# Attention by pairs of heads: logits of two heads in turn, probabilities divided by their sums before they are transposed

## The chip, the core and the metric

One core of a Trainium2 chip runs the whole program in one launch. The metric is the device time of that launch in microseconds, of which lower is better. Three runs of the kernel before took 1363.26, 1365.01 and 1368.75 us, median 1365.01.

## The reference, cut to what matters

Two transformer blocks of two layers each, over 256 tokens of width 1024, in float32. Three of the four mixers are attention with 16 heads of 64 channels:

```python
# causal attention of layer 0 ("moba"; with one block of 256 keys it is plain causal attention)
l = einsum('hqd,hkd->hqk', q, k) * scale
l = where(d >= 0, l + bias_table[bucket(d)], NEG)
o = einsum('hqk,hkd->hqd', softmax(l), v)
# layer 1 ("dsa"): the same, and each query keeps the 64 keys of the highest index score
logits = where(valid, logits + bias, NEG);  p = softmax(logits)
# layer 3, dilated: three branches (window, dilation) = (128,1), (512,4), (2048,16);
# their outputs are joined by their log-sum-exp, so that one softmax over all three holds
```

The rest is matrix products: gated or squared-relu MLPs, a short convolution, projections.

## The kernel before

All weights, 424 chunks of 512 KB, stream from memory in the order of their use (`Stream`, lines 96 to 134). Each chunk holds eight 128x128 tiles. ScalarE (ACT) rounds it to float32r (`wH`, line 121), VectorE (DVE) subtracts to get the rest (`wL`, line 122), in quarters of 128x256. Each product of a tile is then three matmuls (`mm3` and `mm3t`, lines 202 to 214: high by high, high by low, low by high). Matmuls of attention itself are plain float32 (`mm`, line 216), which the trace shows as two records each.

`Kernel.attend` (lines 505 to 530) issues attention as a pipeline over units. A unit is one head in the two causal layers (16 units, class `Causal`) and one head and one half of the queries in the dilated layer (32 units, class `Dilated`). In turn i it issues, in this order: `qk` of unit i (logits, into one PSUM bank of the pool `psB`, which has four), `soft` of unit i, some pieces of background work, `tr` of unit i - lag (three 128x128 transposes on TensorE (PE), and a copy by DVE from PSUM to the tile `ptS`), further pieces, `pv` of unit i - lag - 1 and `fin` of unit i - lag - 2. The background `bg` is the generator of the projections that feed attention and of the output projection that follows it; a table of numbers gives the pieces per turn. One piece is 12 matmuls of a projection, with the weights that they need. A scheduler then fixes each engine's order; instructions of an engine run in that order.

`soft_part` (line 1087) is one DVE instruction that adds the bias, negates, and keeps the row's least value (line 1093), and one `Exp` on ACT that also sums the row (line 1094). The division by that sum comes at the end, for two heads together, since a pair of heads fills the 128 rows of one output tile: `inverses` (line 1106) takes the reciprocals on DVE and spreads them over 64 columns on ACT (line 1112); `pv` (line 1114) transposes them on PE (line 1123), copies them out of PSUM on ACT (line 1125), does the products with the values, multiplies by them on DVE (line 1128, tile `ao`), and splits the result into high and low parts (`split_into`, lines 223 and 224).

The two heads of a pair, e = 0 and 1, have their queries and keys in rows 0 to 63 and 64 to 127 of one tile, so a logits matmul uses 64 rows of the array. `select_keys` (line 783) in layer 1 has such matmuls too: for the second half of the queries two per bank, in the order bank 0 and bank 1 of e = 0, bank 0 and bank 1 of e = 1 (lines 789 to 797).

## Time and profile before

| what | value |
|---|---|
| runs, median | 1365.01 us |
| profiled execution: time of the run | 1363.71 us |
| its span, first to last instruction | 1361.9 us |
| mean granted TensorE clock | 0.991 |
| busy: PE / PE weight loads / DVE / ACT / GpSimd (POOL) | 98% / 90% / 69% / 62% / 1% |
| weight and other DMA traffic | 238.73 MB, 175 GB/s mean |

The profiled execution is one run, so sums over it are set against 1363.71 us, of which 1361.9 us is its span. PE records are pipelined: a record's duration covers its way through the array, and records overlap. What a matmul costs a busy PE is the distance from its start to the next one's start. DVE and ACT records overlap by some 0.08 us in the same way.

### The profile page before, as it was taken

How to read it: one execution, taken by the hardware profiler on the slowest of the kernel's cores; microseconds unless marked ns; L12 is line 12 of the kernel's file. 1: busy time of each engine (PE TensorE's matmuls, PEld its weight loads, DVE VectorE, ACT ScalarE, POOL GpSimd, SP SyncE). 2: the span in 40 equal slices, each digit the busy share in tenths (PEclk: the TensorE clock that was granted, in tenths of full speed). 3: DMA queues.
4: the chain of work that ended last, by engine and by line, in shares of the span. 5: the costliest groups of instructions: out<-in, count | busy, mean ns of one | idle time of the engine just before them, and what ended most of it. 6: DMA issues, size and time to landing. Idle time of an engine off the chain costs nothing.

```text
span 1361.9 us, 27454 instructions
## 1 busy us (share of the span) xinstructions
PE 1335.7 (98%) x10238; PEld 1230.3 (90%) x10238; DVE 946.1 (69%) x2529; ACT 841.2 (62%) x2325; POOL 7.4 (1%) x17
## 2 busy tenths in 40 slices
PE   8899999999999999999999999999999999999998
PEld 6788999999779999999989999888998987899997
DVE  6467866568878656689886666775677777766665
ACT  6466856566767656586675555777655555655554
POOL 0000000000000000000000000000000000000000
PEclk9899999999899999999999999999999999999999
DMA  8933565655224665656656666465755553466662
GB/s 238 267 109 110 171 200 173 203 180 176 92 79 140 192 211 186 203 163 216 203 168 202 196 190 194 152 211 186 222 191 162 156 158 109 142 204 194 192 196 77
DMA packets 67137, 238.73 MB, mean 175 GB/s; under 512 B 8139, under 2 KB 8556, under 8 KB 67004
## 3 DMA queue, kind: packets, MB, share of 16 engines
q1 hardware_dynamic: 65324, 231.30, 54.0%
q0 software_dynamic: 1536, 5.64, 1.8%
q8 instruction: 80, 1.31, 0.4%
q14 instruction: 53, 0.43, 0.1%
q10 hardware_dynamic: 144, 0.06, 0.0%
HBM read 228.83 MB, written 1.84 MB: 169 GB/s over the span
## 4 chain that ended last, share of the span: by engine, by line
PE 92%; DVE 3%; DMA 2%; ACT 2%; issue 0%; DVEq 0%; ACTq 0%
PE A L205 18%; PE A L206 17%; PE A L207 17%; PE B L217 7%; PE B L206 4%; PE B L205 4%; PE B L207 4%; PE B L213 3%; PE B L214 3%; PE B L212 3%; PE A L212 2%; PE A L214 2%; PE A L213 2%; DMA wT<-in_w 2%; PE B L1162 1%; PE B L1204 1%
## 5 line engine op out<-in xcount | busy, mean ns | idle before, releaser
L121 ACT ACTIVATE wH<-wT 128x256 fp32r<-128x256 f32 x1696 | 574.8, 406 | 400.5 <-PE A L206 177.4
L122 DVE TENSOR_TENSOR wL<-wT,wH 128x256 fp32r<-128x256 f32 x1696 | 617.4, 419 | 278.7 <-ACT wH L121 277.4
L205 PE MATMUL A<-Xh,wH 128*128 128x256 f32 x1768 | 492.4, 279 | 0.7 <-DVE x L386 0.7
L206 PE MATMUL A<-Xl,wH 128*128 128x256 f32 x1768 | 491.9, 278 | 0.3 <-DVE Xl L227 0.2
L207 PE MATMUL A<-Xh,wL 128*128 128x256 f32 x1768 | 491.5, 278 | 0.0
L205 PEld LDWEIGHTS A<-Xh,wH 128*128 128x128 f32 x1768 | 333.7, 189 | 3.1 <-ACT Xh L226 1.0
L206 PEld LDWEIGHTS A<-Xl,wH 128*128 128x128 f32 x1768 | 333.7, 189 | 2.1 <-DVE Xl L227 1.0
L207 PEld LDWEIGHTS A<-Xh,wL 128*128 128x128 f32 x1768 | 333.6, 189 | 0.0
L206 PE MATMUL B<-Al,wH 128*128 128x256 f32 x512 | 142.3, 278 | 0.0
L205 PE MATMUL B<-Ah,wH 128*128 128x256 f32 x512 | 142.1, 278 | 0.0
L207 PE MATMUL B<-Ah,wL 128*128 128x256 f32 x512 | 142.1, 278 | 0.0
L205 PEld LDWEIGHTS B<-Ah,wH 128*128 128x128 f32 x512 | 96.2, 188 | 0.0
L206 PEld LDWEIGHTS B<-Al,wH 128*128 128x128 f32 x512 | 96.1, 188 | 0.0
L207 PEld LDWEIGHTS B<-Ah,wL 128*128 128x128 f32 x512 | 95.9, 187 | 0.0
L214 PE MATMUL B<-wL,Fh 128*128 128x512 f32 x176 | 69.4, 394 | 0.0
L213 PE MATMUL B<-wH,Fl 128*128 128x512 f32 x176 | 69.0, 392 | 0.0
L212 PE MATMUL B<-wH,Fh 128*128 128x512 f32 x176 | 68.4, 389 | 0.0
L1094 ACT ACTIVATE pr<-pr,sm 128x128 f32<-128x128 f32 (+1 forms) x96 | 48.1, 501 | 25.4 <-DVE sm L1093 24.7
L205 PE MATMUL A<-XQh,wH 128*128 128x256 f32 x192 | 58.0, 302 | 0.0
L212 PE MATMUL A<-wH,Xh 128*128 128x512 f32 x128 | 51.8, 405 | 5.8 <-ACT wH L121 5.4
L206 PE MATMUL A<-XQl,wH 128*128 128x256 f32 x192 | 53.6, 279 | 0.0
L207 PE MATMUL A<-XQh,wL 128*128 128x256 f32 x192 | 53.4, 278 | 0.0
(252 smaller groups left out, 1700.1 us busy)
## 6 DMA issues: line engine op xcount, KB each, us to landing
wT<-in_w SPq DMA_DIRECT2D x422, 512.0 KB, 3.7
sw<-raw SPq DMA_DIRECT2D x48, 128.0 KB, 2.6
bias<-ud POOLq DMA_DIRECT2D x4, 512.0 KB, 13.6
wT<-in_w SPq DMA_DIRECT2D x4, 256.0 KB, 3.9
out_dram<-xt SPq DMA_DIRECT2D x4, 256.0 KB, 2.4
x<-in_x SPq DMA_DIRECT2D x3, 256.0 KB, 5.9
ud<-us POOLq DMA_DIRECT2D x1, 768.0 KB, 10.2
growfinal_norm<-in_gr POOLq DMA_DIRECT2D x1, 512.0 KB, 5.7
```

What stands on the lines that cost most here:

```text
L121: nc.scalar.activation(h[:, at], t[:, at], AF.Copy)
L122: nc.vector.tensor_tensor(out=lo[:, at], in0=t[:, at], in1=h[:, at], op=ALU.subtract)
L205: mm(out, lhsT=wh, rhs=xh, start=start, stop=False, skip_group_check=True)
L206: mm(out, lhsT=wh, rhs=xl, start=False, stop=False, skip_group_check=True)
L207: self.last = mm(out, lhsT=wl, rhs=xh, start=False, stop=stop, skip_group_check=True)
L212: mm(out, lhsT=xh, rhs=wh, start=start, stop=False, skip_group_check=True)
L213: mm(out, lhsT=xl, rhs=wh, start=False, stop=False, skip_group_check=True)
L214: self.last = mm(out, lhsT=xh, rhs=wl, start=False, stop=stop, skip_group_check=True)
L217: self.nc.tensor.matmul(out, lhsT=lhsT, rhs=rhs, start=start, stop=stop, skip_group_check=True)
L1094: nc.scalar.activation(p, p, AF.Exp, scale=-1.0, bias=mx, accum_out=s["l"][:, i, self.e:self.e + 1])
L1162: K.nc.tensor.transpose(pt[:, i * P:(i + 1) * P], self.p[:, i * P:(i + 1) * P], K.ident[:])
L1204: K.nc.tensor.transpose(pt[:, b * P:(b + 1) * P], self.p[:, b * P:(b + 1) * P], K.ident[:])
```

## The change

Attention goes by pairs of heads. A causal unit is now a pair (8 units); a dilated unit is a pair and one half of the queries (16 units). `qk` takes two banks and issues the two heads' matmuls alternately, e = 0 and 1. The probabilities are multiplied by the reciprocal sums before they are transposed: in the causal layers on DVE, issued one turn after the softmax (`norm_late`), in the dilated layer on GpSimd, issued in the turn of the softmax (`norm_early`). The spread, transposed and copied reciprocals of `inverses` and `pv` and the multiplication into `ao` go; the product's bank is split directly. The first matmul of a product now opens its accumulation. The tables of pieces are rewritten for the longer turns, and causal `pr` tiles have 6 buffers for 4.

```diff
@@ attend
             at(i, "qk")
+            at(i - 1, "norm_late")
             at(i, "soft")
             some(m // 2)
+            at(i, "norm_early")
             at(i - lag, "tr")
             ...
-            self.spent(4)
+            self.spent(6)
@@ moba
-        self.attend([Causal(self, h, qk, v, OH, OL, done) for h in range(H)], bg, lambda i: 2 if i < 11 else 1 if i < 16 else 2)
+        self.attend([Causal(self, hp, qk, v, OH, OL, done) for hp in range(KT)], bg, lambda i: 4 if i < 5 else 2 if i < 8 else 4)
@@ dsa
-        self.attend([Causal(self, h, qk, v, OH, OL, done, sel) for h in range(H)], bg, lambda i: 1 if i < 5 else 0 if i < 8 else 1, 2)
+        self.attend([Causal(self, hp, qk, v, OH, OL, done, sel) for hp in range(KT)], bg, lambda i: 2 if i < 2 else 0 if i < 4 else 2, 2)
@@ dilated
-        units = [Dilated(self, u // 2, u % 2, qk, v0, v12, OH, OL, done) for u in range(2 * H)]
-        self.attend(units, bg, lambda i: 3 if i < 25 else (i % 3 > 0) if i < 32 else 2)
+        units = [Dilated(self, u // 2, u % 2, qk, v0, v12, OH, OL, done) for u in range(H)]
+        self.attend(units, bg, lambda i: 6 if i < 12 else 3 if i < 13 else 2 - i % 2 if i < 16 else 4)
@@ class Attention
+    def norm(self, eng):
+        nc, K = self.K.nc, self.K
+        n = len(self.parts)
+        r = K.lt([P, 2, n], "ar", 4)
+        nc.vector.reciprocal(r, self.l)
+        for e in range(2):
+            for j, at in enumerate(self.parts):
+                eng.tensor_scalar(self.p[e][:, at], self.p[e][:, at], r[:, e, j:j + 1], None, op0=ALU.mult)
...
-    def inverses(self):
-        nc, K = self.K.nc, self.K
-        s = self.shared()
-        r = K.lt([P, 2, 2], "ar", 4)
-        nc.vector.reciprocal(r, s["l"])
-        s["r"] = rx = K.lt([P, 2, 2, 64], "arow", 3)
-        nc.scalar.activation(rx, r.unsqueeze(3).to_broadcast([P, 2, 2, 64]), AF.Copy)
 
     def pv(self):
...
-        for i in range(2):
-            nc.tensor.transpose(b[:, S + i * P:S + (i + 1) * P], rx[:, i, :, :].rearrange("p a b -> p (a b)"), K.ident[:])
-        rows = K.lt([P, S], "arow", 3)
-        nc.scalar.activation(rows, b[:, S:2 * S], AF.Copy)
-        self.products(b, [s["pt", e] for e in range(2)])
-        o = K.lt([P, S], "ao", 2)
-        nc.vector.tensor_tensor(out=o, in0=b[:, 0:S], in1=rows, op=ALU.mult)
-        K.split_into(self.OH[:, hp, :], self.OL[:, hp, :], o[:])
+        self.products(b, self.pts())
+        K.split_into(self.OH[:, self.hp, :], self.OL[:, self.hp, :], b[:, 0:S])
@@ class Causal, qk
-        self.lg = lg = K.bankB()
-        K.mm(lg[:, 0:P], q[:, 0:P], k[:, 0:P], True, False)
-        K.mm(lg[:, P:P + S], q[:, P:S], k[:, 0:S], False, self.sel is None)
+        self.lg = [K.bankB() for _ in range(2)]
+        for i, (to, of, nk) in enumerate(((slice(0, P), slice(0, P), P), (slice(P, P + S), slice(P, S), S))):
+            for e in range(2):
+                K.mm(self.lg[e][:, to], self.half(q, e)[:, of], self.half(k, e)[:, 0:nk], i == 0, i == 1 and self.sel is None)
@@ class Causal
+    parts = (slice(0, P), slice(P, P + S))
+    def norm_late(self):
+        self.norm(self.K.nc.vector)
@@ class Dilated, qk
+        for e in range(2):
+            q0, k0 = (self.half(t, e) for t in ops[0])
+            K.mm(self.lg[e][:, 0:S], q0[:, i * P:(i + 1) * P], k0, True, False)
         for n in range(2):
-            for f in range(2):
-                at = slice((2 * i + f) * 64, (2 * i + f + 1) * 64)
-                q, k = (q1, k1) if n == f else (q2, k2)
-                K.mm(lg[64 * f:64 * f + 64, S + 64 * n:S + 64 * n + 64], q[:, at], k[:, at], False, f == 1 and n == 1)
+            for e in range(2):
+                for f in range(2):
+                    at = slice((2 * i + f) * 64, (2 * i + f + 1) * 64)
+                    q, k = (self.half(t, e) for t in ops[1 if n == f else 2])
+                    K.mm(self.lg[e][64 * f:64 * f + 64, S + 64 * n:S + 64 * n + 64], q[:, at], k[:, at], False, f == 1 and n == 1)
@@ class Dilated
+    parts = (slice(0, 384),)
+    def norm_early(self):
+        self.norm(self.K.nc.gpsimd)
```

Three places show what moves. First TensorE in the dilated layer, the logits of one unit. The names are the bank `B` that is written, and the tiles `raw` (a branch's queries and keys) that are read. Before:

```order
L217 MATMUL B_13027<-raw_12485 128x256
L217 MATMUL B_13027<-raw_12485 64x64
L217 MATMUL B_13027<-raw_12640 64x64 x2
L217 MATMUL B_13027<-raw_12485 64x64
L205 MATMUL A_13002<-XQh,wH_13004 128x256
```

and after the change:

```order
L217 MATMUL B_13345<-raw_12932 128x256
L217 MATMUL B_13346<-raw_12932 128x256
L217 MATMUL B_13345<-raw_12932 64x64
L217 MATMUL B_13345<-raw_13138 64x64
L217 MATMUL B_13346<-raw_12932 64x64
L217 MATMUL B_13346<-raw_13138 64x64
L217 MATMUL B_13345<-raw_13138 64x64
L217 MATMUL B_13345<-raw_12932 64x64
```

One head's five matmuls in one bank become two heads' ten in two banks, side by side in the order; there are 16 such groups where there were 32.

Second, TensorE in layer 1, in the stretch of the pipeline that has no background work. `kf` and `qf` are keys and queries, `sel` the mask of the chosen keys, `pr` the probabilities, `arow` the spread reciprocals. Before:

```order
L1162 MATMUL B_4858<-ident,pr_4808 128x128 x3
L1123 MATMUL B_4864<-ident,arow_4838 128x128 x2
L217 MATMUL B_4877<-kf_4416,qf_4417 128x128
L217 MATMUL B_4877<-kf_4416,qf_4417 128x256
L217 LDWEIGHTS identb
L217 MATMUL B_4877<-sel_4419,identb 128x384
```

and after the change:

```order
L1114 MATMUL B_4834<-ident,pr_4719 128x128 x3
L1114 MATMUL B_4840<-ident,pr_4720 128x128 x3
L217 MATMUL B_4845<-kf_4384,qf_4385 128x128
L217 MATMUL B_4845<-kf_4384,qf_4385 128x256
L217 MATMUL B_4846<-kf_4384,qf_4385 128x128
L217 MATMUL B_4846<-kf_4384,qf_4385 128x256
```

The transposes of the reciprocals are gone, and two heads' logits stand next to each other in two banks; here the scheduler has put both matmuls of one head ahead of the other's.

Third, VectorE in the same stretch. `ar` are the reciprocals, `al` the sums. Before:

```order
L1110 RECIPROCAL ar_4940<-al_4851 128x4
L1163 COPY ptS_4948<-B_4944 128x384
L122 TENSOR_TENSOR wL_5234<-wT_5232,wH_5233 128x256
L1128 TENSOR_TENSOR ao_4925<-B_4916,arow_4919 128x256
L1093 ISA pr_4954,sm_419_4956<-B_4950,bias 128x128
```

and after the change:

```order
L1105 RECIPROCAL ar_4901<-al_4861 128x4
L122 TENSOR_TENSOR wL_5201<-wT_5199,wH_5200 128x256
L224 TENSOR_TENSOR OL_4673<-B_4886,OH_4672 128x256
L1108 TENSOR_SCALAR pr_4859<-pr_4859,ar_4901 128x128
L1108 TENSOR_SCALAR pr_4859<-pr_4859,ar_4901 128x256
L1108 TENSOR_SCALAR pr_4860<-pr_4860,ar_4901 128x128
L1108 TENSOR_SCALAR pr_4860<-pr_4860,ar_4901 128x256
L1091 ISA pr_4907,sm_386_4910<-B_4893,bias 128x128
```

Four multiplications of the probabilities stand between the reciprocals and the next pair's softmax, where before there was the one multiplication into `ao`. In the dilated layer GpSimd gets 32 multiplications of 128x384, two after each reciprocal.

## Rows read from the trace of the kernel before

**Rows 1.** The first part of the page: busy time, share of the span and count of instructions, by engine.

```profile
PE 1335.7 (98%) x10238; PEld 1230.3 (90%) x10238; DVE 946.1 (69%) x2529; ACT 841.2 (62%) x2325; POOL 7.4 (1%) x17
```

**Rows 2.** Busy time by stretch: from:to and length, then busy us (count) of PE, weight loads, DVE, ACT, POOL, then the granted clock, the share of the DMA engines and GB/s. The stretches are attention of layer 0 from the first softmax on, the start and the rest of that of layer 1, most of the dilated attention, and eight units within it.

```profile
82.90:124.30 41.40, 41.34 (x293) 31.57 (x291) 32.55 (x126) 30.32 (x107) 0.00 (x0) 1.00 0.23 75
364.40:381.50 17.10, 17.10 (x110) 12.00 (x110) 13.02 (x56) 15.35 (x49) 0.00 (x0) 1.00 0.29 93
381.50:420.00 38.50, 38.35 (x302) 32.52 (x301) 26.29 (x92) 23.07 (x77) 0.00 (x0) 1.00 0.32 100
980.80:1126.90 146.10, 146.10 (x1305) 130.76 (x1304) 111.04 (x261) 79.72 (x221) 0.00 (x0) 1.00 0.54 165
1040.03:1089.28 49.25, 49.25 (x446) 44.06 (x445) 37.30 (x88) 26.10 (x74) 0.00 (x0) 1.00 0.54 161
```

**Rows 3.** Who waited for whom in 980 to 1162 us: total us, times, longest us. The longest of all, and two of PE's.

```profile
ACT wH L121 <- issue: 31.1, 18, 2.6
...
PEld B L217 <- issue: 12.0, 39, 0.4
...
PEld B L1204 <- ACT pr L1094: 0.5, 2, 0.3
```

**Rows 4.** The chain that ended last, within 1047 to 1066 us: start, us on the chain, what. L205 to L207 are background matmuls, L217 x10 one unit's logits, L1204 its transposes, L1123 the transposes of the reciprocals.

```profile
1047.41 1.00 PE B L217 x10
1048.41 0.32 PE A L205
...
1050.02 0.33 PE B L1204 x3
...
1058.78 1.00 PE B L217 x10
...
1064.46 0.22 PE B L1123 x2
```

**Rows 5.** Instructions of PE in order of time, in layer 1: start, us until the last one ends, then line and tiles. The next row's start shows what a group cost PE.

```profile
375.56 0.92 PE L217 MATMUL B<-kf,qf 64*128 64x128 f32 x4
376.41 0.87 PE L217 MATMUL B<-ptS,v 128*64 128x256 f32 x8
377.21 0.34 PE L217 MATMUL B<-sel,identb 128*128 128x384 bf16 x1
377.39 0.49 PE L1162 MATMUL B<-ident,pr 128*128 128x128 f32 x3
377.71 0.38 PE L1123 MATMUL B<-ident,arow 128*128 128x128 f32 x2
378.02 0.92 PE L217 MATMUL B<-kf,qf 64*128 64x128 f32 x4
...
379.47 0.92 PE L217 MATMUL B<-kf,qf 64*128 64x128 f32 x4
```

**Rows 6.** The score matmuls of `select_keys` (tile `kidx`, 64 rows, 256 columns) in two stretches: from:to and length, busy us (count) of PE, weight loads and DVE, clock, DMA share, GB/s. The first holds the matmuls of one bank (two, in four records), the second those of two banks, which belong to rows 0 to 63 and 64 to 127.

```profile
345.67:346.44 0.77, 0.76 (x4) 0.67 (x4) 0.00 (x0) 1.00 0.00 0
347.60:348.38 0.78, 0.77 (x8) 0.71 (x8) 0.00 (x0) 1.00 0.07 21
```

**Rows 7.** Instructions of DVE in order of time, the softmax of two heads in layer 0.

```profile
82.93 0.28 DVE L1093 CUSTOM_DVE_ANT_0 pr<-B,bias 128x128 f32<-128x128 f32 x1
...
83.14 0.42 DVE L1093 CUSTOM_DVE_ANT_0 pr<-B,bias 128x256 f32<-128x256 f32 x1
...
83.48 0.28 DVE L1093 CUSTOM_DVE_ANT_0 pr<-B,bias 128x128 f32<-128x128 f32 x1
```

**Rows 8.** Groups of DVE instructions in 364 to 412 us: busy us, mean ns of one, idle us before them.

```profile
L1163 DVE COPY ptS<-B 128x384 f32<-128x384 f32 x16 | 8.8, 550 | 0.1
L224 DVE TENSOR_TENSOR OL<-ao,OH 128x256 fp32r<-128x256 f32 x7 | 3.0, 424 | 0.5 <-ACT OH L223 0.5
L1128 DVE TENSOR_TENSOR ao<-B,arow 128x256 f32<-128x256 f32 x7 | 3.0, 424 | 7.9 <-PE B L217 7.9
L1110 DVE RECIPROCAL ar<-al 128x4 f32<-128x4 f32 x8 | 1.4, 174 | 0.0
```

**Rows 9.** DVE instructions by a scalar, from and to SBUF, with ns min/median/max: in the rotary tables with a scalar per row (L939) and a constant (L942), and in `select_keys` at 128 and 256 columns (L817).

```profile
L939 DVE TENSOR_SCALAR ang<-posf,consts x1: 344/344/344, 644.0 to 644.0; 128x256 f32<-128x256 f32 x1
L942 DVE TENSOR_SCALAR turns<-ang x1: 285/285/285, 644.6 to 644.6; 128x256 f32<-128x256 f32 x1
...
L817 DVE TENSOR_SCALAR sel<-sc x2: 206/244/282, 362.5 to 363.4; 128x128 bf16<-128x128 f32 x1, 128x256 bf16<-128x256 f32 x1
```

**Rows 10.** The compute instructions of GpSimd in the whole program: busy us, mean ns.

```profile
masks.py:199 POOL TENSOR_SCALAR_AFFINE_SELECT ident<-ident 128x128 f32<-128x128 f32 x1 | 0.3, 290 | 0.1
masks.py:197 POOL MEMSET ident<- 128x128 f32 x1 | 0.2, 205 | 0.3 <-POOLq L1309 0.3
L1309 POOL MEMSET const-uint8-127<- 128x1 uint8 x1 | 0.1, 103 | 0.0
```

**Rows 11.** Groups of DVE instructions in 980.8 to 1126.9 us, as in rows 8.

```profile
L122 DVE TENSOR_TENSOR wL<-wT,wH 128x256 fp32r<-128x256 f32 x147 | 54.8, 418 | 18.9 <-ACT wH L121 18.9
L1093 DVE CUSTOM_DVE_ANT_0 pr<-B,consts 128x384 f32<-128x384 f32 x24 | 13.3, 553 | 7.4 <-PE B L217 7.1
...
L1021 DVE TENSOR_TENSOR sw<-sw,sn 128x1024 f32<-128x1024 f32 x9 | 10.9, 1217 | 0.0
```

More of the change, by code (lines that the diff above doesn't have):

```diff
@@ L1116, in pv @@
             return
[L1117 to L1120 removed]
+        K = self.K
         b = K.bankB()
[L1122 to L1127 removed]
@@ L1163, in tr, with pts @@
-        K.nc.vector.tensor_copy(self.transposed([P, 3 * P], 4), pt[:, 0:3 * P])
+        self.pt = []
+        for e in range(2):
+            t = K.lt([P, 3 * P], "ptS", 4)
+            K.nc.vector.tensor_copy(t, self.turned(e))
+            self.pt.append(t)
+    def pts(self):
+        return self.pt
     def products(self, b, pts):
@@ L1179, in __init__ @@
+    def __init__(self, K, hp, i, qk, v0, v12, OH, OL, done):
+        super().__init__(K, hp, qk, OH, OL, done)
         self.i, self.v0, self.v12 = i, v0, v12
-        self.last = self.e == 1 and i == 1
+        self.last = i == 1
     def qk(self):
         K, i = self.K, self.i
-        (q0, k0), (q1, k1), (q2, k2) = [[t[self.rows, :] for t in self.qk_[(b, self.h // 2)]] for b in range(3)]
-        self.lg = lg = K.bankB()
-        K.mm(lg[:, 0:S], q0[:, i * P:(i + 1) * P], k0, True, False)
@@ L1198, in tr, with norm_early @@
+        for e in range(2):
+            self.soft_part(self.lg[e][:, 0:384], self.p[e][:], K.c[:, C_MASK + 384 * i:C_MASK + 384 * i + 384], self.l[:, e, :])
+    def norm_early(self):
+        self.norm(self.K.nc.gpsimd)
     def tr(self):
         K, i = self.K, self.i
-        if self.last:
-            self.inverses()
-        pt = K.bankB()
-        for b in range(3):
-            K.nc.tensor.transpose(pt[:, b * P:(b + 1) * P], self.p[:, b * P:(b + 1) * P], K.ident[:])
-        t = self.transposed([P, 3, S], 3)
@@ L1206, in tr, with pts @@
-        K.nc.vector.tensor_copy(t[:, :, i * P:(i + 1) * P], pt[:, 0:384].rearrange("p (a b) -> p a b", a=3))
+        s = K.heads.setdefault(self.hp, {})
+        for e in range(2):
+            if e not in s:
+                s[e] = K.lt([P, 3, S], "ptS", 3)
+            K.nc.vector.tensor_copy(s[e][:, :, i * P:(i + 1) * P], self.turned(e).rearrange("p (a b) -> p a b", a=3))
+    def pts(self):
+        return self.K.heads[self.hp]
     def products(self, b, pts):
```

79 lines of the change are left out of this document (35 added, 44 removed).

## The prediction

> **What bounds it now.** The first part of the page comes first: TensorE is busy 98% of the span, VectorE 69%, GpSimd 1% [rows 1]. Such a mean may hide stages with other limits, so the attention stretches are read one by one [rows 2]: TensorE is busy 41.34 of 41.40 us in layer 0, 17.10 of 17.10 and 38.35 of 38.50 in layer 1, all of 146.10 in the dilated layer, at a granted clock of 1.00 throughout. The table of waits for the dilated layer says the same from the other side: ScalarE and VectorE wait long, for buffers and for each other, while TensorE's wait for an exponential is 0.5 us, in 2 places, and the 12.0 us of its weight loads before products end on nobody [rows 3]. The chain of waits there is TensorE from row to row [rows 4]. So a microsecond of TensorE's time taken out of attention is a microsecond off the end, as long as no other engine becomes the bound. VectorE is the one to watch: 32.55 of 41.40 us in layer 0, 13.02 of 17.10 at the start of layer 1, 111.04 of 146.10 in the dilated layer [rows 2].
>
> **What TensorE saves.**
>
> *Logits.* A causal head's four records cost TensorE 0.85 us (375.56 to 376.41) [rows 5], a dilated unit's ten 1.00 us [rows 4]. Each uses 64 rows of the array. The score matmuls of `select_keys` show what such halves do when they are issued for two banks: 8 records of both halves fill 0.78 us where 4 records of one half fill 0.77 [rows 6]. So the second head should be free. 32 heads become 16 pairs: 16 x 0.85 = 13.6 us. 32 dilated units become 16: 16 x 1.00 = 16.0 us. In layer 1 the order keeps one head's two matmuls together; the rows of `select_keys` have that order too, so it should not matter. Unshown is whether the small 64x64 matmuls, which use a quarter of the array, go four at a time; if the heads don't overlap in them, about 0.43 us (1.00 less 256 columns at the causal head's 0.85 for 384) comes back 16 times, 6.9 us.
>
> *Transposes of the reciprocals.* 24 output tiles (8 + 8 + 8) x 0.22 us [rows 4] = 5.3 us; the 0.31 us from 377.71 to 378.02 [rows 5] would make it 7.4. I take the first, since it has background work behind it, as most have.
>
> *Change-over.* The first background matmul behind a group of logits costs 0.32 us [rows 4], against 0.11 to 0.12 for its followers: 0.2 us less for each group that goes, 16 x 0.2 in the dilated layer, and 0.1 each for 16 causal ones, many of which have none behind them: 4.8 us. The products, the transposes of the probabilities and the weights stay.
>
> If TensorE stays the bound everywhere, that is 13.6 + 16.0 + 5.3 + 4.8 = **39.7 us**.
>
> **What VectorE takes back in the causal layers.** Per pair it loses `ao`, 0.42 us as a record and 0.34 by distance (records overlap by 0.08) [rows 8], and gains four multiplications. Their nearest row is the one of 256 columns with a scalar per row, 0.344 us; with a constant it is 0.285, and 128 columns against 256 take 0.206 against 0.282 [rows 9]. That makes 0.26 and 0.19 by distance, 0.45 a head, 0.92 a pair with rounding. The reciprocals stay (0.17 a record, 0.09 by distance) [rows 8]. So VectorE has 0.58 us more per pair, 9.3 us over 16 pairs. A head's softmax takes 0.56 us of it (82.93 to the next head's start at 83.48) [rows 7].
>
> Whether that shows depends on the stretch. In layer 0 VectorE would have 32.55 + 8 x 0.58 = 37.2 us in a stretch for which TensorE needs 41.4 - 8 x (0.85 + 0.22 + 0.1) = 32.0: the attention lasts 37.2, and 5.2 us of the saving are lost. In layer 1 four pairs have no background work. Such a pair costs 3.91 us now (375.56 to 379.47) [rows 5]. TensorE would need 0.85 for logits, 0.36 for the masks, 0.66 for transposes [rows 4] and 0.80 for products, 2.7 us. VectorE has softmax 1.12, reciprocals 0.09, multiplications 0.92, two copies 2 x 0.47 and `OL` 0.34 [rows 8], 3.4 us, and one weight cut of 0.34 (0.418 as a record [rows 11]): 3.8 us. So a pair saves 0.1 us where TensorE alone would save 1.2: 4 x 1.1 = 4.4 lost. The other pairs of layer 1 have 12 to 24 background matmuls, so TensorE stays the bound there. Together **9.6 us lost**; the bounds are 0 (VectorE moves its weight cuts to before or behind the stretch, since TensorE waits only for those that are late) and the whole causal gain, 13.6 + 16 x 0.22 + 1.6 = 18.7.
>
> ScalarE only loses work (the spread and the copy, 24 times), and the weights' transfers keep their place in SP's queue; both cost nothing, since TensorE waits for neither now.
>
> **What GpSimd costs in the dilated layer.** It gets 32 multiplications of 128x384; no row shows one. Its rows are a memset of 128 columns in 0.205 us against one column in 0.103, which is 0.8 ns a column, and an affine select of 128 columns in 0.290, which is 1.5 [rows 10]: for 384 columns 0.42 to 0.67 us as estimates, and 0.87 at three times the affine select. I take 0.7. They hide: eight units, four turns of the new kind, take 49.25 us [rows 2], and after the change 49.25 - 4 x 1.2 - 2 x 0.22 = 44.0, 11.0 a turn. Transposes of a turn come a turn after its logits, while softmax of two heads (2 x 0.55) [rows 11], `Exp`, reciprocal and two multiplications take some 4 to 4.5 us. Only the last units, 4 to 6 us apart with little background, lack the cover. VectorE in those four turns loses two `ao` and gains two reciprocals: 36.8 of 44.0 us, 1.8 us free a turn. I take **2 us lost** for queueing; the bounds are 0 and 9.6 (below).
>
> Here is a row to weigh. Half of VectorE's work in this layer has two operands in SBUF: the weights' cuts, 54.8 us [rows 11], and the rotations by tables such as the row of 1217 ns [rows 11]. GpSimd's multiplications read SBUF at the same time, and no row shows the two at once. By the Trainium skill, "SBUF — State Buffer", section "Who interferes with whom", a VectorE instruction with two SBUF inputs contends with a GpSimd instruction that reads SBUF, and the one that comes first blocks the other fully. By that rule VectorE would stand still during both multiplications of a turn, 0.84 to 1.7 us, which the 1.8 us free would just hold, so that the sum would be the same by it unless a multiplication is longer; the case where it is longer is the second rival.
>
> **Sum.** 39.7 - 9.6 - 2 = 28.1 us. 1363.71 - 28.1 = 1335.6 for the profiled execution's like; the median of the runs stands 1.3 us above it: **1337 us**. For this case alone 1328 to 1343: the causal loss halved or 1.4 times as large, and the 6.9 us of the small matmuls.
>
> **The rivals.**
>
> *VectorE becomes the bound in all of causal attention* and eats the 18.7 us: 39.7 - 18.7 - 2 = 19.0, 1346 us. For it speaks that four multiplications stand right before the next softmax in VectorE's order, so the next exponential and transposes queue behind them; against it that 12 or more background matmuls per pair in most of layer 1 give TensorE 1.4 us more. 0.16.
>
> *GpSimd and VectorE hinder each other.* If a multiplication takes 1.2 us and VectorE stands still meanwhile, it needs 2.4 us of 1.8 free, 0.6 x 16 = 9.6 us lost: 39.7 - 9.6 - 9.6 = 20.5, 1345 us. It decides from 0.9 us a multiplication. For it: the large share of two-operand work [rows 11]; against it the times of rows 10. The skill's rule above ("SBUF — State Buffer") speaks for it. 0.15. Both of these rivals together end at 1354.
>
> *TensorE stays the bound everywhere*: 39.7, 1325 us (with the upper 7.4 us for the transposes 1323). For it: VectorE has slack before and behind the causal stretches. 0.10.
>
> *The halves don't run side by side*, and logits cost what they did: 5.3 + 4.8 - 2 = 8, 1357 us; the causal layers are TensorE's again. Against it stand rows 6. 0.05.
>
> *Slower: GpSimd becomes the bound.* The place is the dilated turn: two multiplications must fit into 11.0 us, so it binds from 5.5 us each, and the rest of the gain is gone where (2T - 11.0) x 16 = 30, at 6.4 us. At 7 us: 48 - 30, 1383 us. That would be 18 ns a column, against at most 1.5 in rows 10. 0.03.
>
> *It doesn't do what it says*: the scheduler or the banks (two for logits of four) hold a turn back as long as the logits took, about 1365 us. Two logits banks leave two for transposes and products, where one unit left three. 0.04.
>
> **How the numbers follow.** The forecast has 0.47. The range 1323 to 1354 leaves out the last three cases and the far ends of the first. A measurement can tell some 0.5%, 7 us, from no change: the forecast and the next three rivals are faster by more, the halves' case mostly, in all 0.91; same 0.06; slower 0.03.
>
> **What would show it.** Ten logits of two heads should fill about 1.0 us of TensorE in the dilated layer and a causal pair's 0.85, with the heads' records starting within nanoseconds of each other; 1.4 there means the small matmuls took turns, 2.0 that the halves don't overlap. The rows of the spread, the transposed and copied reciprocals and `ao` must be gone. In layer 0's attention VectorE should be busy above nine tenths and TensorE idle before transposes, waiting for the probabilities; a stretch of 32 us refutes that. In the dilated layer the duration of GpSimd's multiplication, the mean of the weights' cut against 418 ns, and TensorE's idle time before transposes with GpSimd named decide the second rival and the slower one. I am wrong if the dilated layer gains under 10 us or the causal layers gain over 17.

## The result and the profile after

The changed kernel takes 1330.3 us (median of four runs, 1328.53 to 1331.86) where the kernel before took 1366.88 on the same chip (1363.26 to 1373.22): a ratio of 0.9746, 95% interval 0.9717 to 0.9775. The forecast was 1337 in 1323 to 1354. The profiled execution after took 1328.53 us with a span of 1326.6, against 1363.71 and 1361.9: 35.3 us less span, where the sum said 28.1.

The first part of the page after, and GpSimd's new group of part 5:

```profile
PE 1295.1 (98%) x10190; PEld 1204.7 (91%) x10190; DVE 950.0 (72%) x2577; ACT 824.2 (62%) x2277; POOL 55.8 (4%) x49
...
L1108 POOL TENSOR_SCALAR pr<-pr,ar 128x384 f32<-128x384 f32 x32 | 48.3, 1521 | 200.9 <-DVE ar L1105 185.0
```

Against [rows 1], TensorE lost 40.6 us of busy time and is still at 98%; VectorE's total hardly moved (946.1 before), ScalarE lost 17 us. GpSimd's multiplication takes 1.52 us, twice what the prediction took.

To see where the time came from, both traces are cut at the same places of the program: ScalarE rounds 1696 quarter chunks in the same order in both, so the start of the n-th rounding is a mark. The stretches from mark 72 to 168, 408 to 480 and 1264 to 1464 hold the attention of layers 0, 1 and 3. These are the stretches of before, then of after (columns as in [rows 2]):

```profile
59.20:157.80 98.60, 98.12 (x761) 86.42 (x760) 71.96 (x226) 66.15 (x204) 0.00 (x0) 0.99 0.42 132
325.80:424.30 98.50, 97.21 (x689) 80.94 (x688) 76.14 (x270) 64.72 (x191) 0.00 (x0) 0.97 0.35 108
975.40:1185.80 210.40, 207.60 (x1751) 180.11 (x1750) 157.95 (x378) 115.42 (x325) 0.54 (x1) 0.99 0.51 158
```

```profile
58.90:148.70 89.80, 88.89 (x743) 80.57 (x743) 74.83 (x250) 59.75 (x187) 0.00 (x0) 1.00 0.44 144
316.30:408.50 92.20, 88.01 (x673) 74.98 (x672) 78.68 (x294) 58.11 (x175) 0.00 (x0) 0.98 0.36 115
958.90:1151.00 192.10, 187.83 (x1735) 169.06 (x1734) 156.19 (x378) 110.11 (x308) 48.91 (x33) 0.98 0.58 174
```

8.8 + 6.3 + 18.3 = 33.4 us come from the three layers, 1.9 from the rest of the program. A second trace of the changed kernel (e11, below) gives 8.7 + 3.3 + 18.4 = 30.4. TensorE is still busy in nearly all of layer 0 and the dilated layer. In layer 1 it has 4.2 us without work, where before it had 1.3, and VectorE is busy 78.68 of 92.20 us: there the forecast bound shows in part.

The same stretches by kind of matmul, each record counted from its start to the start of TensorE's next one (so a wait falls to the record ahead of it), in us, summed from the traces:

```
                       layer 0          layer 1          dilated
                    before  after    before  after    before  after
logits               13.13   6.42     13.61   9.41     33.38  16.92
reciprocals           2.14   0         2.22   0         2.32   0
transposes            5.83   5.02      4.80   6.18      8.76  10.98
masks                 -      -         2.50   3.97      -      -
products with values  6.41   6.98      6.42   6.41     11.82  11.83
all other            71.09  71.25     69.00  66.23    154.12 152.44
```

Nearly all of it is the logits, 27.4 us, and the reciprocals, 6.7; transposes and masks give 4.3 back, since waits and the lower clock fall to them and to the logits of layer 1. The logits of a causal pair and of a dilated group, with the row behind each (timeline of TensorE after; start, us until the last record ends):

```profile
93.93 0.93 PE L217 MATMUL B<-k,q 64*128 64x128 f32 x8
94.79 0.39 PE L205 MATMUL A<-OH,wH 128*128 128x256 f32 x1
...
1038.46 1.09 PE L217 MATMUL B<-raw 64*128 64x256 f32 x20
1039.49 0.39 PE L205 MATMUL A<-XQh,wH 128*128 128x256 f32 x1
```

Two causal heads take 0.86 us, where one took 0.85 [rows 5], and twenty dilated records 1.03, where ten took 1.00 [rows 4]. The single records of that dilated group start in clusters: two 7 ns apart while the 256 columns run, then four within 20 ns. So the 64x64 matmuls do go four at a time.

### The profile page after: what moved, and what is told of

It reads as the page before. It is cut to its first block, busy times and chain, and to the rows that moved or that the text cites. A ratio compares the mean times of both kernels' runs of the same rounds, so it can differ in the third digit from the quotient of the medians.

```text
span 1326.6 us, 27425 instructions
## 1 busy us (share of the span) xinstructions
PE 1295.1 (98%) x10190; PEld 1204.7 (91%) x10190; DVE 950.0 (72%) x2577; ACT 824.2 (62%) x2277; POOL 55.8 (4%) x49
## 4 chain that ended last, share of the span: by engine, by line
PE 90%; DVE 4%; ACT 2%; DMA 1%; issue 1%; POOL 0%; SPq 0%; DVEq 0%; ACTq 0%; POOLq 0%
PE A L205 18%; PE A L206 18%; PE A L207 18%; PE B L217 5%; PE B L206 4%; PE B L205 4%; PE B L207 4%; PE B L214 3%; PE B L213 3%; PE B L212 3%; PE A L212 2%; PE A L214 2%; PE A L213 2%; PE B L1114 2%; DVE wL L122 1%; DMA wT<-in_w 1%
## 5 line engine op out<-in xcount | busy, mean ns | idle before, releaser
L205 PE MATMUL A<-Xh,wH 128*128 128x256 f32 x1768 | 492.4, 279 | 0.7 <-DVE x L386 0.7
L207 PE MATMUL A<-Xh,wL 128*128 128x256 f32 x1768 | 490.8, 278 | 0.0
L205 PEld LDWEIGHTS A<-Xh,wH 128*128 128x128 f32 x1768 | 333.5, 189 | 3.5 <-ACT Xh L226 1.0
L207 PEld LDWEIGHTS A<-Xh,wL 128*128 128x128 f32 x1768 | 333.8, 189 | 0.0
L205 PE MATMUL B<-Ah,wH 128*128 128x256 f32 x512 | 142.1, 278 | 0.0
L207 PE MATMUL B<-Ah,wL 128*128 128x256 f32 x512 | 142.1, 278 | 0.0
L205 PEld LDWEIGHTS B<-Ah,wH 128*128 128x128 f32 x512 | 96.2, 188 | 0.0
L207 PEld LDWEIGHTS B<-Ah,wL 128*128 128x128 f32 x512 | 95.9, 187 | 0.0
L1108 POOL TENSOR_SCALAR pr<-pr,ar 128x384 f32<-128x384 f32 x32 | 48.3, 1521 | 200.9 <-DVE ar L1105 185.0
L205 PE MATMUL A<-XQh,wH 128*128 128x256 f32 x192 | 55.6, 290 | 0.0
L207 PE MATMUL A<-XQh,wL 128*128 128x256 f32 x192 | 53.4, 278 | 0.0
```

The costliest lines, as they stand in the source:

```text
L205: mm(out, lhsT=wh, rhs=xh, start=start, stop=False, skip_group_check=True)
L207: self.last = mm(out, lhsT=wl, rhs=xh, start=False, stop=stop, skip_group_check=True)
L1108: eng.tensor_scalar(self.p[e][:, at], self.p[e][:, at], r[:, e, j:j + 1], None, op0=ALU.mult)
```

## The experiments

Stretches and spans are of each run's trace, in us; the ratio is to the kernel before on the same chip, with its interval. The rest of the program varies by itself from 952.5 to 961.2 (the last section says by what), so the verdicts go by the stretches. The spans of e1, e3, e5, e7, e8, e9 and e11 lie outside all that was expected for them, and e10's fits its rival alone; in e8, e9 and e10 the rest is 6 to 9 us longer than in the changed kernel.

```
                     layer 0  layer 1  dilated    rest    span   ratio
before                  98.6     98.5    210.4   954.4  1361.9
changed                 89.8     92.2    192.1   952.5  1326.6  0.9746 [0.9717, 0.9775]
e1_same_rows            94.6     94.5    199.1   959.7  1347.8  0.9854 [0.9823, 0.9885]
e2_heads_apart          88.9     92.3    203.7   959.5  1344.4  0.9837 [0.9809, 0.9865]
e3_norm_at_end          90.9     93.5    195.2   955.4  1334.9  0.9787 [0.9749, 0.9825]
e4_no_norm_causal       87.5     90.0    192.1   954.0  1323.6  0.9710 [0.9678, 0.9742]
e5_no_norm_dilated      90.3     92.1    190.2   954.2  1326.8  0.9765 [0.9742, 0.9787]
e6_dilated_on_dve       88.3     93.6    189.3   954.9  1326.1  0.9761 [0.9736, 0.9786]
e7_pool_x4              90.5     93.7    249.5   953.7  1387.4  1.0215 [1.0191, 1.0238]
e8_causal_on_pool       96.3     94.1    192.0   958.8  1341.3  0.9836 [0.9803, 0.9868]
e9_small_apart          89.6     91.9    192.8   961.2  1335.6  0.9796 [0.9760, 0.9832]
e10_no_gpsimd           90.4     93.3    189.0   961.2  1334.0  0.9734 [0.9706, 0.9763]
e11_changed_again       89.9     95.2    192.0   953.9  1331.0  0.9763 [0.9737, 0.9789]
e12_norm_causal_x2      94.4     96.9    191.3   953.8  1336.5  0.9820 [0.9771, 0.9870]
```

The changed kernel run twice agrees within 0.1 us in layer 0 and the dilated layer, and differs by 3.0 in layer 1. Runs that leave the code of a stretch as it is say more: layer 0 takes 88.3 to 90.5 us in seven traces (changed, e5, e6, e7, e9, e10, e11), layer 1 91.9 to 95.2 in six (changed, e5, e6, e7, e9, e11), the dilated layer 191.3 to 192.1 in five (changed, e4, e8, e11, e12). So a difference under some 2 us in layer 0, 3 in layer 1 and 1 in the dilated layer tells nothing by itself. In layer 1 most of it goes with the granted clock: the columns of [rows 2] for this layer in e4, e5, e11 and e12:

```profile
314.70:404.70 90.00, 86.70 (x673) 74.24 (x672) 71.31 (x254) 57.76 (x174) 0.00 (x0) 1.00 0.38 118
317.80:409.90 92.10, 86.90 (x673) 74.26 (x672) 78.54 (x294) 57.98 (x174) 0.00 (x0) 1.00 0.38 115
316.70:411.90 95.20, 91.57 (x673) 77.75 (x672) 78.85 (x294) 57.78 (x174) 0.00 (x0) 0.95 0.35 111
320.80:417.70 96.90, 90.84 (x673) 76.28 (x672) 86.14 (x326) 57.95 (x174) 0.00 (x0) 0.95 0.35 108
```

### Is it the rows? (e1)

```diff
     def half(self, t, e):
-        return t[64 * e:64 * e + 64]
+        return t[0:64]
```

> The changed kernel, with both heads of a pair reading queries and keys in rows 0 to 63 of their tile (so the second head's result is the first head's); order, banks and counts stay. If the second head is free because its half of the rows runs beside the first's, it must now cost its full time: a dilated group of logits 2.0 us for 1.09 (16 groups, 16 us), a causal pair 1.7 for 0.86 (16 pairs, 13.6 us, part of it behind VectorE in layer 1). Span 1349 to 1356 us against 1326.6. Rival (the gain came from fewer groups, change-overs and transposes, not from the rows): below 1332.

A causal pair and a dilated group (timeline of TensorE, with the row behind each):

```profile
97.67 1.57 PE L217 MATMUL B<-k,q 64*128 64x128 f32 x8
99.17 0.38 PE L205 MATMUL A<-OH,wH 128*128 128x256 f32 x1
...
1056.68 1.74 PE L217 MATMUL B<-raw 64*128 64x256 f32 x20
1058.35 0.39 PE L205 MATMUL A<-XQh,wH 128*128 128x256 f32 x1
```

1.50 and 1.67 us, against 0.86 and 1.03: the rows are the main cause. The three stretches grow by 14.1 us; by TensorE's starts the logits alone take 50.3 us, against 32.8 in the changed kernel and 60.1 before, so the rows carry 17.6 of the 27.4 us saved. All this is less than expected, and the difference teaches something: two heads one after the other in the same rows do not cost twice a single head (1.70 and 2.00). The first and the last matmul of a run of one shape cost extra (before, the two 256-column records of a head start 0.32 and 0.31 us ahead of the next record; in e1 the inner ones 0.22), and a group of two heads pays that once. So of the 0.97 us that a dilated pair saved, 0.33 came from grouping alone and 0.64 from the rows.

### Is it the order? (e2, e9)

e2 issues all matmuls of head 0 ahead of all of head 1; e9 does so for the 64x64 ones alone:

```diff
@@ Dilated.qk, e2 (Causal.qk alike)
         for e in range(2):
             q0, k0 = (self.half(t, e) for t in ops[0])
             K.mm(self.lg[e][:, 0:S], q0[:, i * P:(i + 1) * P], k0, True, False)
-        for n in range(2):
-            for e in range(2):
+            for n in range(2):
@@ Dilated.qk, e9
-        for n in range(2):
-            for e in range(2):
+        for e in range(2):
+            for n in range(2):
```

> The changed kernel, with all logits matmuls of one head issued ahead of the other head's, in all layers. Theory 1 (matmuls start in order, so the second head can only overlap the tail of the first): 0.12 us a pair in layer 0, as layer 1 shows in that order (0.985 for 0.862), and 0.1 to 0.5 us a group in the dilated layer: span 1329 to 1336 us. Theory 2, the prediction's (the order doesn't matter as long as the two heads stand next to each other): 1325 to 1328. Rival (only alternation makes halves run side by side): 16 us or more, over 1343.

> The changed kernel; in the dilated logits the two heads' 128x256 matmuls still alternate, but the four 64x64 ones of head 0 come ahead of the four of head 1. Theory 1 (TensorE starts a matmul of the other half ahead of its place when it stands two matmuls behind, as it did in the causal layers with heads apart, but not four or five): the small ones take 0.21 us a group more, 16 times, span 1329 to 1332 us. Theory 2 (what kept the heads apart in the dilated layer was the change from 64x64 to 64-row matmuls of full width between them, which no longer stands there): as the changed kernel, a group 1.02 us, span 1325 to 1328.

The dilated group in e2, and a causal pair of layer 0:

```profile
92.97 0.93 PE L217 MATMUL B<-k,q 64*128 64x128 f32 x8
93.83 0.39 PE L205 MATMUL A<-Xh,wH 128*128 128x256 f32 x1
...
1050.62 2.08 PE L217 MATMUL B<-raw 64*128 64x256 f32 x20
1052.62 0.38 PE L205 MATMUL A<-XQh,wH 128*128 128x256 f32 x1
```

And the dilated group in e9:

```profile
1047.01 1.11 PE L217 MATMUL B<-raw 64*128 64x256 f32 x20
1048.05 0.39 PE L205 MATMUL A<-XQh,wH 128*128 128x256 f32 x1
```

In the causal layers the order is indifferent, as the prediction had read from [rows 6]: 0.86 us (0.89 in two pairs), the second head's first record 13 ns behind the first head's, though a 256-column matmul of head 0 stands between them in the order. In the dilated layer the same edit undoes everything: 2.00 us, no overlap at all. The stretch is 11.6 us longer than in the changed kernel, and by TensorE's starts its logits are 15.4 us longer (32.3 for 16.9); the faster pace of the last section and a higher granted clock (0.99 for 0.98) give some of that back. No theory on record for e2 had this split. e9 tells why: with the wide matmuls alternating and the small ones apart, a group takes 1.04 us, as with all of them alternating, so four matmuls of distance are not too many. What stood between the heads in e2's dilated group and in none of the other three cases is a change of shape: head 1's 256-column matmul had to follow head 0's 64x64 ones. So the overlap seems to end at a change between 64x64 and full-width tiles; a limit at exactly five matmuls of distance would do the same and is not excluded. By the Trainium skill, "TensorEngine Tiling (Array Packing)", section "Key Properties", a change of the tiling mode drains the engine; the traces agree, 2.00 us against 1.04. The span of e2 alone, 1344.4 us, would have confirmed the rival for the wrong reason: 7 us of it lie outside the three stretches, as 9 of e9's do.

### What is the early division worth? (e3)

e3 keeps pairs and alternating logits and puts the old end back: reciprocals spread, transposed, copied, and a multiplication into `ao`.

```diff
-    def norm_late / norm_early: self.norm(...)
+    (nothing)
@@ pv
+        for i in range(2): nc.tensor.transpose(b[:, S + i * P:S + (i + 1) * P], rx[:, i, :, :]..., K.ident[:])
+        nc.scalar.activation(rows, b[:, S:2 * S], AF.Copy)
         self.products(b, self.pts())
+        nc.vector.tensor_tensor(out=o, in0=b[:, 0:S], in1=rows, op=ALU.mult)
```

> Pairs of heads and logits in turn as in the changed kernel, but the division by the sums as in the kernel before: reciprocals spread, transposed and copied, and the product multiplied on VectorE. This is the logits' part of the change alone. If that part is nearly all of it and the early division adds the 24 transposes of reciprocals (6.7 us by TensorE's starts before) less its waits: span 1329 to 1333 us against 1326.6. By the prediction's sum (early division costs 9.6 + 2 and gives 5.3) it would be faster than the changed kernel: 1320 to 1322.

By the stretches e3 keeps 7.7 + 5.0 + 15.2 = 27.9 us of the gain, and the early division adds 1.1 + 1.3 + 3.1 = 5.5, of which only the dilated layer's 3.1 is clear of what unchanged code varies by. Little of this need be the transposes: in e3 the products, which wait for the copied reciprocals (`arow`), stand between the logits of five dilated pairs and several causal ones, which stand together in the changed kernel. One dilated pair of e3:

```profile
1010.57 1.09 PE L217 MATMUL B<-raw 64*128 64x256 f32 x18
1012.04 1.55 PE L217 MATMUL B<-ptS,v 128*64 128x256 f32 x24 [0.38 <-ACT arow L1139]
1013.52 0.32 PE L217 MATMUL B<-raw 64*64 64x64 f32 x2
```

By TensorE's starts the logits so take 37.9 us in e3 for 32.8, 5.1 us more; how much of that is the old end and how much the order that the scheduler chose was not taken apart. By its own terms the early division comes out about even: 6.7 us of transposes saved, some 4.5 and 1.9 lost (the next two sections). The prediction's sum made it a loss of 6.3 (5.3 gained, 9.6 and 2 lost), which no run shows. The rewritten tables of pieces and the two more `pr` buffers are in every run after the change; their share was not tried.

### What do VectorE's multiplications cost? (e4, e12)

```diff
@@ Causal.norm_late
-        self.norm(self.K.nc.vector)
+        pass                              # e4
+        self.norm(self.K.nc.vector, 2)    # e12: each multiplication done twice
```

> The changed kernel without reciprocals and multiplications in the two causal layers (the probabilities stay undivided there). What VectorE's multiplications cost there comes back. By TensorE's idle time in the trace of the changed kernel, some 3 us in layer 1 and 0.5 in layer 0, and the lower clock that follows it: span 1320 to 1324 us against 1326.6. By the size in the prediction, 9.6 us: 1317. If VectorE's share costs nothing: 1326.

> The changed kernel with each of the causal layers' multiplications on VectorE done twice (the probabilities of these layers are divided twice). VectorE gets 16 x 0.92 = 14.7 us more, half of it in each layer. The prediction's sizing (VectorE is the bound of all of layer 0's attention and of four pairs of layer 1, so that its work adds to the end in full there): 7.4 us more in layer 0 (its stretch 97 us for 89.8) and 3.7 in layer 1. Theory now (leaving the first set out gave back 2.3 and 2.2 us by stretch, a third of its 7.4, since VectorE moves weight cuts out of the tight places): with the slack used up it costs more than the first set, but less than in full in layer 0: 3 to 6 us there, 3 to 5 in layer 1.

Without them layer 0 takes 2.3 us less and layer 1 2.2: **some 4.5 us, not 9.6**. Against all traces with the changed kernel's code, layer 0's part is 0.8 to 3.0. In layer 1 e5 and e9, at the same granted clock of 1.00, took 92.1 and 91.9 us for e4's 90.0, so its 2 us hold. Done twice, the multiplications cost 4.6 and 4.7 us more. In layer 0 that is twice the first set, and TensorE is idle 3.3 us there for 0.9: some slack was there and is then used up. In layer 1 most of the 4.7 goes with the clock: at the same granted clock of 0.95, without the extra work, e11 took 95.2 us, so e12's 96.9 is 1.7 more, under the 3 to 5 expected. VectorE's groups in layer 0's attention of the changed kernel, from the first softmax to the last product (79.8 to 124.2 us):

```profile
L122 DVE TENSOR_TENSOR wL<-wT,wH 128x256 fp32r<-128x256 f32 x34 | 12.2, 419 | 0.0
L1091 DVE CUSTOM_DVE_ANT_0 pr<-B,bias 128x128 f32<-128x128 f32 (+1 forms) x32 | 9.6, 354 | 1.5 <-PE B L217 1.5
...
L1108 DVE TENSOR_SCALAR pr<-pr,ar 128x128 f32<-128x128 f32 (+1 forms) x32 | 8.0, 317 | 0.0
```

The multiplications were sized well: 0.317 us each, 0.24 by distance, 0.95 a pair for 0.92. What failed is the sentence that they lengthen the stretch in full. VectorE did its 32 multiplications and 34 weight cuts there, but in its tightest part, 82 to 115 us, only 10 cuts: it had done more of them ahead, VectorE was busy 28.72 of these 33 us, less than the nine tenths that the prediction had named as its test, and TensorE was idle 0.9 us in the whole of layer 0, 0.5 of it before transposes.

In layer 1 the bound is there at the start. The start of its attention, after, by stretch:

```profile
352.00:356.00 4.00, 2.94 (x27) 2.44 (x26) 4.00 (x19) 3.57 (x7) 0.00 (x0) 1.00 0.00 0
356.00:360.00 4.00, 4.00 (x35) 2.69 (x33) 4.00 (x18) 3.85 (x13) 0.00 (x0) 1.00 0.70 180
360.00:363.60 3.60, 2.23 (x14) 1.61 (x13) 3.60 (x23) 2.79 (x13) 0.00 (x0) 0.95 0.65 237
363.60:366.90 3.30, 3.15 (x15) 1.88 (x13) 3.16 (x17) 1.70 (x9) 0.00 (x0) 0.54 0.01 2
```

and TensorE's waits from 344 to 372 us (us, times, longest):

```profile
PE B L1114 <- DVE sm L1091: 1.3, 1, 1.3
PE B L217 <- DVE sel L819: 1.1, 1, 1.1
```

VectorE has no gap from 352 to 363.6 us. TensorE waits for it, and then runs at 0.54 of its clock for 3.3 us, mostly at the 1.2 GHz level, behind 3.6 us in which it had been busy for 2.2. One of the two waits is for the selection of keys (`sel`), not for the softmax, and e4, without the multiplications, still waits 1.6 us in the same place for VectorE: the multiplications lengthen these waits and don't make them alone. The kernel before shows such a fall ahead of its attention, within the selection of keys:

```profile
350.00:355.00 5.00, 4.93 (x17) 3.85 (x18) 4.77 (x16) 1.50 (x4) 0.00 (x0) 0.50 0.26 70
```

At half the clock, half of 5 us is lost there, and near half of 3.3 in the changed kernel. How often the clock falls differs between runs of the same code (0.95 to 1.00 over layer 1), which is why layer 1 says least.

### What does GpSimd cost, and what does it buy? (e5, e6, e7, e8)

```diff
@@ Dilated.norm_early
-        self.norm(self.K.nc.gpsimd)
+        pass                              # e5
+        self.norm(self.K.nc.vector)       # e6
+        self.norm(self.K.nc.gpsimd, 4)    # e7: each multiplication done four times
@@ Causal.norm_late
-        self.norm(self.K.nc.vector)
+        self.norm(self.K.nc.gpsimd)       # e8
```

> The changed kernel without reciprocals and GpSimd multiplications in the dilated layer (the probabilities stay undivided there). The trace of the changed kernel shows TensorE idle 1.2 us before the transposes there, waiting for GpSimd, and the cuts of the weights at 436 ns for 418: span 1324 to 1326 us against 1326.6. Rival (GpSimd and VectorE hinder each other by the 9.6 us of the prediction's second rival): 1317.

> The changed kernel with the dilated layer's multiplications on VectorE in GpSimd's place, in the same turn. VectorE gets 32 x some 0.4 us = 13 us more in a stretch where it is busy 107.8 of 126.0 us, and TensorE stays the bound; GpSimd's latency and the mutual blocking go. If so: span 1324 to 1329 us, with the cuts of the weights back at 418 ns. Rival (VectorE gets late with the weights, which is what GpSimd avoids): 1331 or more.

> The changed kernel with each GpSimd multiplication of the dilated layer done four times (the result is divided four times over). 8 x 1.52 us = 12.2 us a turn against 10.4 to 10.9 that the turn takes: GpSimd becomes the bound there, 1.3 to 1.8 us a turn, 16 turns, and the last units add their latency: span 1348 to 1362 us. Rival (GpSimd's time is hidden whatever it is, since transposes come a turn later): below 1332.

> The changed kernel with the causal layers' multiplications on GpSimd, a turn later as now. By 3.2 ns a column (1.245 us for 384) a pair costs GpSimd 2.5 us where nothing hinders it, and VectorE is 0.9 us a pair lighter. If VectorE's 0.9 us is what costs in layer 1: span 1321 to 1325 us. Rival (the longer way from the softmax to the transposes, 2.5 us for 1.0, costs TensorE more where there is no background work): 1329 to 1336.

Without the division the dilated stretch takes 190.2 us for 192.1: GpSimd costs **1.9 us**, where the prediction took 2. It buys nothing: with the multiplications on VectorE the stretch takes 189.3, and e8 and e12, with GpSimd and at e6's granted clock of 0.99, took 192.0 and 191.3. TensorE's wait for GpSimd's multiplications in the changed kernel's dilated layer, and then VectorE's groups from 966 to 1092 us, one of the changed kernel and two of e6:

```profile
PE B L1114 <- POOL pr L1108: 1.2, 2, 0.8
```

```profile
L122 DVE TENSOR_TENSOR wL<-wT,wH 128x256 fp32r<-128x256 f32 x145 | 55.6, 437 | 13.4 <-ACT wH L121 13.2
```

```profile
L122 DVE TENSOR_TENSOR wL<-wT,wH 128x256 fp32r<-128x256 f32 x144 | 52.4, 419 | 8.6 <-ACT wH L121 8.3
...
L1108 DVE TENSOR_SCALAR pr<-pr,ar 128x384 f32<-128x384 f32 x24 | 9.0, 416 | 0.2
```

VectorE does the job in 0.42 us against 1.52, and its weight cuts take 419 ns, against 437 beside GpSimd: 145 cuts x 0.018 = 2.6 us of VectorE's time that GpSimd's help costs, for 9.0 saved.

e7 is the prediction's slower rival made real, and its mechanism holds, at a lower price: GpSimd is busy 98.2 of the 100 us from 1000 on, TensorE waits 38.9 us for it, and the kernel is 2.15% slower than before (that stretch's row and the wait's).

```profile
1000.00:1100.00 100.00, 89.55 (x855) 81.31 (x855) 75.75 (x170) 48.02 (x134) 98.21 (x64) 0.97 0.56 158
```

```profile
PE B L1114 <- POOL pr L1108: 38.9, 25, 5.8
```

Here two divisions take 8 x 1.52 = 12.1 us a turn. The rival had the gain gone from 2 x 6.4 = 12.8 us a turn, since it counted 11.0 us for every turn; the last four turns, without much background, are 4 to 6 us long, and the mean granted clock from 1100 to 1200 us was 0.82. e7 lost 57 us in the stretch where 21 to 35 were expected; that these two make up the difference was not taken apart.

e8 speaks against GpSimd in layer 0, which takes 96.3 us for 89.8 (layer 1's 94.1 is within what unchanged code takes). TensorE waits there before each of the eight pairs' transposes, 4.4 us in all, and its granted clock falls to 0.83 from 80 to 100 us, a loss of some 3 us that the changed kernel does not have:

```profile
80.00:100.00 20.00, 16.08 (x102) 10.61 (x100) 10.41 (x54) 12.87 (x50) 10.47 (x14) 0.83 0.16 49
```

### A version without GpSimd (e10, e11)

```diff
@@ Dilated.norm_early
-        self.norm(self.K.nc.gpsimd)
+        self.norm(self.K.nc.vector)
@@ Causal.tr
-            K.nc.vector.tensor_copy(t, self.turned(e))
+            if self.sel is not None and e:
+                K.nc.scalar.activation(t, self.turned(e), AF.Copy)
+            else:
+                K.nc.vector.tensor_copy(t, self.turned(e))
```

> The changed kernel with the dilated layer's multiplications on VectorE, and in layer 1 one of the two copies of the transposed probabilities per pair on ScalarE for VectorE. The dilated stage should take 189.3 us as without GpSimd, for 192.1, and layer 1, where VectorE is busy without a gap at the start and all of its multiplications together are worth 2.2 us, 1 to 2 us less: span 1321 to 1325 us against 1326.6, ratio to the changed kernel 0.996 to 0.999. Rival (ScalarE's copy holds back its exponentials, or the gain is given back by the lower clock elsewhere): 1326 or more.

> The changed kernel once more, on the chip of these runs: 1328 to 1332 us, span 1325 to 1329, stages as in its first trace within 1 us where the granted clock is the same.

e10's median is 1327.13 us, the changed kernel's on the same chip 1331.99. The profiled run of e10 took 1336.1 (its trace has the slower pace of the last section), its other five 1325.84 to 1327.30, all below the changed kernel's lowest, 1330.96. The two ratios to the kernel before overlap (0.9706 to 0.9763, 0.9737 to 0.9789), so the 5 us are likely, not proven. The dilated stretch, 189.0 for 192.0, is where the trace shows a gain; in layer 1 the copy on ScalarE shows none (93.3, where e6 took 93.6). e11's stretches agree with the first trace within 0.1 us but for layer 1, at the lower clock shown above.

## Why the prediction was right, and where its sizes were off

- **TensorE's time as the bound** held: its saving of 38.4 us (27.4 logits, 6.7 reciprocals, 4.3 in all other matmuls, part of that by clock and pace) less 4.8 given back became some 33.4 us of shorter stretches, 15.1 in the causal layers (12.0 in e11) and 18.3 in the dilated one, on the right side of both limits that the prediction had set itself.
- **Logits**, 29.6 forecast, 27.4 measured. Layer 0 (6.7 for 6.8) and the dilated layer (16.5 for 16.0) are as worked out; in layer 1 only 4.2 of 6.8, since waits and the lower clock fall into the same rows. The reason given, halves side by side, carries some two thirds of it in the dilated layer (e1: 0.64 of 0.97 us a pair); the rest is the ends of a run of matmuls, paid once for two heads, which the prediction did not count as part of what a pair saves. "It should not matter" of the order held where it was said, in the causal layers, and would not have held in the dilated layer (e2).
- **Reciprocals**, 5.3 forecast, 6.7 measured (0.28 us a tile, between the two values of the text).
- **Change-over**, 4.8 forecast, some 1.3 measured. The 0.32 us of [rows 4] is time on the chain; from start to start the first background matmul behind a group of logits takes 0.22 to 0.24 us, 0.11 to 0.12 over its followers, and in the three stretches there are 28 such matmuls before and 19 after.
- **VectorE in the causal layers**: the mis-sized term. 9.6 us forecast, some 4.5 measured (e4). In layer 0 the step failed that sets VectorE's work in a stretch equal to its length; the bound named beside it, cuts moved ahead, was nearer. In layer 1 the mechanism is there (no gap in VectorE for 11.6 us, TensorE waiting 2.4), at about half the size, and the selection of keys has a part in it.
- **GpSimd**: 2 us forecast, 1.9 measured (e5). The 2 was a choice between 0 and 9.6, so that it hit is luck in part. The multiplication takes 1.52 us, not 0.7; at the least it takes 1.24, 3.2 ns a column, twice the affine select's price of [rows 10]. It stayed hidden because a turn leaves room, as the text said, and TensorE's two waits for it, 1.2 us, stand at 1108.7 and 1113.1 us, among the last units, which the text had named.
- **The rule weighed** (the Trainium skill, "SBUF — State Buffer", section "Who interferes with whom"): there is contention, of another size than the rule gives. Both suffer; VectorE never stands still for a whole multiplication, GpSimd does so for nearly a whole rotation. (Of VectorE's work there nearer four fifths than the half of the text has two operands in SBUF: 54.8 us of cuts and three kinds of rotation like the 10.9 of [rows 11], of 111.0.) GpSimd's and VectorE's rows of one such place:

```profile
989.95 3.92 POOL L1108 TENSOR_SCALAR pr<-pr,ar 128x384 f32<-128x384 f32 x2 [6.11 <-DVE ar L1105]
```

```profile
990.02 1.22 DVE L1024 TENSOR_TENSOR raw<-raw,sw 128x1024 f32<-128x1024 f32 x1
991.16 1.01 DVE L1221 COPY ptS<-B 128x384 f32<-128x384 f32 x2
992.09 0.42 DVE L122 TENSOR_TENSOR wL<-wT,wH 128x256 fp32r<-128x256 f32 x1
```

GpSimd's record starts 0.07 us ahead, yet the rotation with its two operands in SBUF ran in its usual 1.22 us, and the first multiplication took 2.32 us for 1.24: it lost 1.08 us. (The records don't show which of the two was first at SBUF.) Of the 69 weight cuts that overlap a multiplication, ten took 718 to 730 ns for 420, a loss of 0.31 us, and none took longer. By the second rival's sum, two multiplications of 1.52 us less the 1.8 us free in each of 16 turns, 20 us would have been lost; 1.9 were.

- **The other rivals**: TensorE as the bound everywhere (1325 us) is nearer to the measured 1330.3 than the forecast of 1337 is. By the stretches the 33.4 us lie midway between its 39.7 and the forecast's 28.1, and e4 and e5 show that some 6.4 us are lost to the other engines, which this rival put at nothing. VectorE as the bound of all causal attention fell (e4), as did halves that take turns (e1), and a change without effect.

In the prediction's own form, the 39.7 us of TensorE's time were 27.4 + 6.7 + 1.3 = 35.4 (layer 1's waits already taken off the logits), and the 11.6 us lost to VectorE and GpSimd some 6.4. Both sizes were too large, one on each side of the sum, and in part they cancelled: that the time came out so near is luck in part. The other 1.9 us of the 35.3 lie outside the change. One line of the prediction does not follow from its own terms: half or 1.4 times the causal loss, and the 6.9 us, give 1332 to 1348 us for the case alone, not 1328 to 1343.

## What to carry to other kernels

Two matmuls that use half of the rows each are worth putting next to each other, when TensorE is the bound: here 27.4 us of logits in a gain of 33.4, some two thirds of it by the rows and a third by fewer groups. (They stood in separate banks; one bank was not tried.) Keep matmuls of one shape together while doing it, since the overlap was gone where the shape of the tile changed between the heads. Before a second engine's added work is charged to a stretch, ask how much of its other work there has to be done there at all; and before work is moved to GpSimd to spare VectorE, set what VectorE would take (0.42 us here) against what GpSimd takes and disturbs (1.52 us, and 18 ns on every weight cut).

## What the runs showed that was not expected

TensorE has two paces at one granted clock. The same 80 us in the MLP behind layer 1, in the changed kernel and in e9, which differs only in the dilated logits:

```profile
480.00:560.00 80.00, 80.00 (x708) 80.00 (x707) 50.44 (x128) 47.47 (x127) 0.00 (x0) 1.00 0.61 198
```

```profile
480.00:560.00 80.00, 80.00 (x682) 80.00 (x681) 49.38 (x123) 46.95 (x125) 0.00 (x0) 1.00 0.60 191
```

Both are full, at a granted clock of 1.00, and one does 708 matmuls where the other does 682 (80 us by the count: one in 113 ns or in 117). Neighbours start every 113 to 114 ns or every 117 to 118, and keep to one of the two for whole stretches of up to 193 us. From mark 480 to 744 that is 186.6 to 186.8 us in eleven of the fourteen traces and 193.2 in e2, e9 and e10. It explains much of the spread of the "rest" (952.5 to 961.2 us), and it is why single runs are compared here by stretches. The stretches are not free of it: over the dilated one the mean distance of neighbouring 128x256 matmuls is 115.4 ns in the changed kernel and 113.7 in e2, some 1.6 us of that stretch. What chooses the pace was not tried.
